# A hybrid decoder block on Trainium2: the way from output projection to gate/up rebuilt, with the memory of gate/up laid out anew

## The chip, the cores and the metric

One core of a Trainium2 chip runs the whole block in one launch. The metric is device time in microseconds (us). Lower is better.

## The reference

Input x is 1024 tokens by 1024 features in float32; there is one layer, with D_FF = 2816.

```
n = _rmsnorm(h, pre_mix_gain[l])
proj = jnp.einsum('bsd,dc->bsc', n, w_in[l])
...
merged = jnp.concatenate([_rmsnorm(a_out, out_norm_a_gain[l]),
                          _rmsnorm(b_out, out_norm_b_gain[l])], axis=-1)
mix = jnp.einsum('bsc,cd->bsd', merged, w_out[l])
h = h + _rmsnorm(mix, post_mix_gain[l])
n2 = _rmsnorm(h, pre_ffn_gain[l])
gu = jnp.einsum('bsd,df->bsf', n2, w_ffn_in[l])
ff = jax.nn.silu(gu[..., :D_FF]) * gu[..., D_FF:]
ff = jnp.einsum('bsf,fd->bsd', ff, w_ffn_out[l])
h = h + _rmsnorm(ff, post_ffn_gain[l])
```

a_out is a gated MLP with position mixing in chunks of 128 tokens, b_out a causal attention with forget gates. The change touches neither.

## The kernel before

**Arithmetic.** Every large product is made in three matmuls on numbers split into a high and a low part: `split` (L112) lets ACT write the rounded high part and DVE the rest, and `mm3` (L117) issues high x high, high x low (the moving operand's low part) and low x high. Names that end in h and l are these parts.

**Stages.** Input projections and attention come first. The output projection follows, token tile by token tile of 128, in the order 0, 1, 6, 7, 2, 4, 3, 5 (L901 to L931). For each tile `merge_start` loads its a and b halves (tile ab), `merge_norm`, `merge_a` and `merge_b` norm, transpose and split them into mh and ml, `mix_chain` makes the two output halves in PSUM (mx), and `mix_tail` (L640) norms them, adds them to x (tile xt), norms the sum again (tile tmp) and stores h. These tiles live in eight slots vs0 to vs7 that the attention's values leave free.

**Gate/up as seven products.** The norm's result and the weights of gate/up are each taken as 2 x 2 blocks, and the 2 x 2 block product is made with seven products of sums in place of eight products. The sums on the side of the activations are the forms n11, n12, n22 (blocks) and s1 to s4 (sums), each 4 x 128 rows by 512 tokens. Token tiles are paired as (0, 6), (1, 7), (2, 4), (3, 5): `norm2_first` (L828) transposes the first tile of a pair and splits n11 and n12, `norm2_second` (L834) transposes the second and makes s1 to s4 and n22. s1 and n22 are split into their forms at once. s2, s3 and s4 go to DRAM (sd) for the first three token pairs, since their place is still taken, and are reloaded before gate/up through three stage buffers (L1003); the fourth token pair is split directly.

**Pairs.** D_FF is covered by 22 steps f, called pairs here, of 128 gate and 128 up columns. `pair_raw` loads a pair's weight blocks (graw), `pair_first` splits two of them (fa), `pair_sums` makes sums (ts), `pair_split` splits these (fbc_0 and fbc_1), `pair_last` splits the fourth block (fd). PE then makes the products in the order 1, 2, 6, 5, 7, 3, 4, each with 4 x 3 = 12 matmuls of 128 x 512. Product 1 opens PSUM bank guA, 2 is guE, 6 adds to guA, 5 opens guC, 7 adds to guA, 3 to guC, 4 to guA. `snapshot` (ACT) copies guA after product 6 (u0), guC after product 5 (u1) and guA after product 7. This order is written out by hand in `pair_start`, `pair_mid` and `pair_end` (L957 on), and the loop at L1083 puts the next pair's loads, sums and splits between them.

```
wform[f, 2], wform[f, 1] = [(hi[:, j], lo[:, j]) for j in range(2)]    # fa
for i, p in enumerate(((6, 5), (7, 4))[j]): wform[f, p] = (hi[:, i], lo[:, i])    # fbc_j
wform[f, 3] = (hi[:, 0], lo[:, 0])    # fd
USES = {1: "n11", 2: "n12", 3: "s4", 4: "n22", 5: "s1", 6: "s2", 7: "s3"}
```

**Memory.** Tiles are allocated from two stacks: the left one grows from the low addresses of each partition, the right one from the high end. Before, the left stack holds s1, n22, n11, n12 and the raw weights and fa of even pairs; the right one holds s2, s3, s4, fbc_0, fbc_1 (three buffers together), fd, ts and the raw weights and fa of odd pairs. So products 5 (s1 with fbc_0) and 4 (n22 with fbc_1) have operands in both stacks in all pairs, and 1 and 2 (n11 and n12 with fa) in odd pairs.

After gate/up the down projection (L1118 on) is made with the same seven products.

## Time and profile before

| what | value |
|---|---|
| runs | 1154.29, 1154.11, 1152.98 us; median 1154.11 |
| profiled execution | 1152.77 us, of which the span is 1151.0 us |
| mean granted clock | 0.99 |
| PE, DVE, ACT, POOL busy | 96%, 63%, 45%, 15% of the span |

The span is what the profile covers, from the first to the last recorded work; the profiled execution's own time is 1.8 us longer. A busy share is an average over the whole span. "Granted clock" is the share of full speed that TensorE was given. A row of the timeline names the engine, the source line, the operation, output<-inputs, and in brackets how long the engine idled before it and what ended that.

### The profile page before, as it was taken

The numbers are of one execution on the slowest core, as the hardware profiler recorded it, in microseconds if no ns is written. First come the engines' busy times: TensorE is split into PE (matmuls) and PEld (weight loads), VectorE is DVE, ScalarE is ACT, GpSimd is POOL, SyncE is SP. The second block draws the span as 40 slices with busy tenths as digits, with TensorE's granted clock in tenths as the row PEclk, the third lists the DMA queues.
The fourth block names the chain that finished last, engine by engine and source line by source line (L and its number), as shares of the span: only waits on it lengthen the run. The fifth ranks groups of instructions, "written<-read, shape, count | busy, mean of one in ns | idle before, by whom it ended". The sixth has DMA issues, their size and how long they took to land.

```text
span 1151.0 us, 15645 instructions
## 1 busy us (share of the span) xinstructions
PE 1110.7 (96%) x5421; PEld 917.1 (80%) x5421; DVE 723.1 (63%) x1288; ACT 512.3 (45%) x989; POOL 176.8 (15%) x247
## 2 busy tenths in 40 slices
...
GB/s 262 60 92 2 83 64 120 83 93 119 75 120 174 115 232 148 110 183 237 204 253 148 181 185 240 161 183 183 230 169 141 198 302 224 196 191 196 197 199 172
DMA packets 85953, 187.76 MB, mean 163 GB/s; under 512 B 9905, under 2 KB 28401, under 8 KB 83058
## 3 DMA queue, kind: packets, MB, share of 16 engines
...
q8 instruction: 43, 0.70, 0.2%
...
## 4 chain that ended last, share of the span: by engine, by line
PE 58%; DVE 2%; issue 1%; POOL 1%; DMA 1%; ACT 1%; DVEq 0%; POOLq 0%; SPq 0%; ACTq 0%
PE guA L118 7%; PE guA L119 7%; PE guA L120 7%; PE guC L120 4%; PE guC L119 4%; PE guC L118 4%; PE dA L118 3%; PE dA L120 3%; PE dA L119 3%; PE dC L118 3%; PE dC L119 3%; PE dC L120 3%; PE guE L118 2%; PE guE L119 2%; PE guE L120 2%; PE mx L120 2%
## 5 line engine op out<-in xcount | busy, mean ns | idle before, releaser
L1141 POOL TENSOR_TENSOR y<-c,gpo 128x512 f32<-128x512 f32 x12 | 20.5, 1734 | 610.2 <-DMA dwr<-ws_d 490.5
L115 DVE TENSOR_TENSOR dal<-dar,dah 128x512 fp32r<-128x512 f32 x77 | 56.4, 733 | 88.2 <-ACT dah L114 88.2
L114 ACT CAST dah<-dar 128x512 fp32r<-128x512 f32 x77 | 48.0, 623 | 104.3 <-PE dC L119 45.8
L119 PE MATMUL dA<-dwl,dah 128*128 128x512 f32 x176 | 70.1, 398 | 2.9 <-DVE dwl L115 2.9
L118 PE MATMUL dA<-dwh,dah 128*128 128x512 f32 x176 | 69.9, 397 | 2.3 <-ACT dah L114 2.3
L120 PE MATMUL dA<-dwh,dal 128*128 128x512 f32 x176 | 69.7, 396 | 0.0
L473 POOL TENSOR_SCALAR sm<-cb,csq 128x128 f32<-128x128 f32 (+3 forms) x64 | 50.3, 787 | 90.2 <-PE pt L508 77.5
L497 ACT ACTIVATE sm<-sm,st 128x128 f32<-128x128 f32 (+3 forms) x64 | 50.0, 781 | 27.7 <-DVE st L493 27.4
L115 DVE TENSOR_TENSOR ptl<-pt,pth 128x512 fp32r<-128x512 f32 (+2 forms) x96 | 51.7, 553 | 10.4 <-ACT pth L114 9.8
L115 DVE TENSOR_TENSOR dwl<-dwr,dwh 128x512 fp32r<-128x512 f32 x77 | 55.4, 720 | 3.2 <-ACT dwh L114 3.2
L114 ACT CAST pth<-pt 128x512 fp32r<-128x512 f32 (+2 forms) x96 | 43.7, 477 | 27.6 <-PE pt L508 27.3
L115 DVE TENSOR_TENSOR fbc_1l<-ts,fbc_1h 128x1024 fp32r<-128x1024 f32 x22 | 26.9, 1225 | 45.9 <-ACT fbc_1h L114 45.9
L118 PE MATMUL qk<-nth,qkw 128*128 128x512 f32 x128 | 53.5, 419 | 0.5 <-DVE k L115 0.4
L118 PE MATMUL mx<-woh,mh 128*128 128x512 f32 x128 | 51.3, 401 | 2.5 <-ACT mh L114 2.5
L491 PE MATMUL s<-k,qu 128*128 128x384 f32 (+4 forms) x192 | 51.1, 365 | 1.5 <-DVE st L493 1.3
L120 PE MATMUL mx<-woh,ml 128*128 128x512 f32 x128 | 50.5, 397 | 1.2 <-DVE ml L115 1.2
L118 PE MATMUL dC<-dwh,dah 128*128 128x512 f32 x132 | 51.3, 389 | 0.0
L119 PE MATMUL dC<-dwl,dah 128*128 128x512 f32 x132 | 51.3, 389 | 0.0
L120 PE MATMUL dC<-dwh,dal 128*128 128x512 f32 x132 | 51.3, 389 | 0.0
L947 ACT COPY u<-guA 128x512 f32<-128x512 f32 x44 | 25.8, 585 | 56.7 <-PE guA L120 56.7
L120 PE MATMUL qk<-nth,qkw 128*128 128x512 f32 x128 | 50.5, 395 | 0.1
L119 PE MATMUL qk<-ntl,qkw 128*128 128x512 f32 x128 | 50.4, 394 | 0.0
...
## 6 DMA issues: line engine op xcount, KB each, us to landing
...
```

The source lines that it names most:

```text
L114: nc.scalar.copy(out=hi, in_=src)
L115: (lo_eng or nc.vector).tensor_tensor(out=lo, in0=src, in1=hi.bitcast(F32), op=ALU.subtract)
L118: nc.tensor.matmul(o, ah, bh, start=first, stop=False, **kw)
L119: nc.tensor.matmul(o, ah, bl, start=False, stop=False, **kw)
L120: nc.tensor.matmul(o, al, bh, start=False, stop=last, **kw)
L473: nc.gpsimd.tensor_scalar(out=sm[:, :n], in0=cbs[hh][:, :n], scalar1=csq[:, hh * NT + i:hh * NT + i + 1], scalar2=1.0, op0=ALU.add, op1=AL ...
L491: nc.tensor.matmul(o[:, :w], qu[:, hl, ts], ks_[hh][:, ks], start=hl == 0, stop=hl == 1)
L497: nc.scalar.activation(sm[:, :n], sm[:, :n], AF.Exp, bias=m, scale=-1.0, accum_out=ssum)
L947: nc.scalar.copy(out=s, in_=o)
L1141: eng.tensor_tensor(out=y[:, cs], in0=src, in1=gpo[:, cs], op=ALU.mult)
```

## The change

**Memory of gate/up.** The left stack now holds s1, s2, n11, n12, fbc_0 (pool wr, one buffer, in the place of the two gains of the norms) and fa of even and odd pairs (pool wq). The right one holds n22, s4, s3, fbc_1 (two buffers), fd, ts and the raw weights (two buffers). Products 1, 2, 6 and 5 then have both operands in the left stack, 7, 3 and 4 both in the right one.

**Output projection to gate/up.** The vs slots are given by a tile's place in the order: xt in 6 and 7, ab in 0 and 1, mh and ml in 2 to 5. The raw weights of pairs 0 and 1 are loaded in halves into slots that come free (`raw_early`), and `pair_first` for both runs before the end of the output projection. The first norm2 step of the last token pair is put inside the last tile's `mix_chain`, and the last `mix_tail` works in halves (`fine`). In `norm2_second` s1 and s2 are split at once, and n22, s4 and s3 go to DRAM; they are reloaded in the order s3, s4, n22. Between product 1 and product 2 of pair 1 the last `norm2_second` is made.

The diff, with unchanged lines left out:

```diff
--- before.py
+++ after.py
+ORDER = [0, 1, 6, 7, 2, 4, 3, 5]
 ...
     def x_load(t):
-        xts[t] = flat(vs_tile(t % 2, f"xt_{t}"))
+        xts[t] = flat(vs_tile(6 + ORDER.index(t) % 2, f"xt_{t}"))
         nc.sync.dma_start(out=xts[t], in_=x[t * P:(t + 1) * P, :])
 ...
-    def mix_tail(t, gains):
+    def mix_tail(t, gains, fine=False):
         oo, xt = [mixo[t, dh] for dh in range(2)], xts[t]
 ...
                                            op0=ALU.mult, op1=ALU.mult)
+        if fine:
+            ss = small(2, "sq")
+            cc = [slice(dh * 512, dh * 512 + 512) for dh in range(2)]
+            for dh, cs in enumerate(cc):
+                nc.vector.tensor_tensor(out=xt[:, cs], in0=xt[:, cs], in1=tmp[:, cs], op=ALU.add)
+                nc.scalar.activation(tmp[:, cs], xt[:, cs], AF.Square, scale=D ** -0.5, accum_out=ss[:, dh:dh + 1])
+            nc.sync.dma_start(out=h_d[t * P:(t + 1) * P, :], in_=xt)
+            r = rstd2(ss)
+            for cs in cc:
+                nc.vector.scalar_tensor_tensor(out=tmp[:, cs], in0=xt[:, cs], scalar=r, in1=gains[1][:, cs],
+                                               op0=ALU.mult, op1=ALU.mult)
+            normed[t] = tmp
+            return
         nc.vector.tensor_tensor(out=xt, in0=xt, in1=tmp, op=ALU.add)
 ...
-    FORMS1, FORMS2 = (("s1", "n22"), ("n11", "n12")), ("s2", "s3", "s4")
+    FORMS1, FORMS2 = (("s1", "s2"), ("n11", "n12")), ("n22", "s4", "s3")
 ...
+    forms = form_tiles(f1_cms[0].__enter__(), FORMS1[0])
+    wr_cm = pool("wr")
+    wr = wr_cm.__enter__()
+    forms.update(form_tiles(f1_cms[1].__enter__(), FORMS1[1]))
+    wq_cm = pool("wq")
+    wq = wq_cm.__enter__()
     sr_cm = pool("sr")
     sr_pools = [(sr_cm.__enter__(), 3)]
 ...
-    forms = {}
-    for cm, names in zip(f1_cms, FORMS1):
-        forms.update(form_tiles(cm.__enter__(), names))
-    wq_cm = pool("wq")
-    wq = wq_cm.__enter__()
-    mx_cm = pool("mix")
-    mx = mx_cm.__enter__()
-    gains = [mx.tile([P, D], F32, tag=nm, name=nm) for nm in ("gpm", "gpf")]
+    gains = [wr.tile([P, D], F32, tag=f"fb0{hl}", name=nm) for hl, nm in (("h", "gpm"), ("l", "gpf"))]
     load_gains(gains)
 ...
     def merge_start(t):
-        a = ab[t] = flat(vs_tile(2 + t % 2, f"ab_{t}"))
+        a = ab[t] = flat(vs_tile(ORDER.index(t) % 2, f"ab_{t}"))
         rows = slice(t * P, (t + 1) * P)
 ...
         b21, b22 = n2_transposed(t, 0, "X"), n2_transposed(t, 1, "O")
-        s1, s2, s3, s4 = [kview(s_tile(f"s{j}_{i}")) for j in range(1, 5)]
-        nc.scalar.copy(out=s1, in_=b21)
-        nc.vector.tensor_tensor(out=s3, in0=b11, in1=s1, op=ALU.subtract)
-        nc.vector.tensor_tensor(out=s1, in0=s1, in1=b22, op=ALU.add)
+        s3, s1, s2, s4 = [kview(s_tile(f"s{j}_{i}")) for j in (3, 1, 2, 4)]
+        nc.scalar.copy(out=s3, in_=b21)
+        nc.vector.tensor_tensor(out=s1, in0=s3, in1=b22, op=ALU.add)
         nc.vector.tensor_tensor(out=s2, in0=s1, in1=b11, op=ALU.subtract)
+        n2_split("s2", s2, cs)
+        n2_split("s1", s1, cs)
+        nc.vector.tensor_tensor(out=s3, in0=b11, in1=s3, op=ALU.subtract)
         nc.vector.tensor_tensor(out=s4, in0=b12, in1=s2, op=ALU.subtract)
         if last:
-            for nm, src in (("s1", s1), ("s2", s2), ("s3", s3), ("s4", s4), ("n22", b22)):
+            for nm, src in (("s3", s3), ("s4", s4), ("n22", b22)):
                 n2_split(nm, src, cs)
             return
-        n2_split("s1", s1, cs)
-        n2_split("n22", b22, cs)
-        for d, src in zip(sd, (s2, s3, s4)):
+        n22 = kview(s_tile(f"n22_{i}"))
+        nc.scalar.copy(out=n22, in_=b22)
+        for d, src in zip(sd, (n22, s4, s3)):
             nc.sync.dma_start(out=d[:, :, cs], in_=src)
 ...
     raws, wform = {}, {}
-    p1_pools = [wq]
+
+    def raw_early(f, half, slot):
+        r = raws[f, half] = flat(vs_tile(slot, f"graw_early_{f}_{half}")).rearrange("p (a w) -> p a w", a=2)
+        nc.sync.dma_start(out=r, in_=io["w_gu"][f, :, 2 * half:2 * half + 2, :])
 ...
     def pair_raw(f):
-        raws[f] = p1_pools[f % 2].tile([P, 4, 512], F32, tag="raw", name=f"graw_{f}", bufs=1)
+        raws[f] = p1.tile([P, 4, 512], F32, tag="raw", name=f"graw_{f}", bufs=2)
         nc.sync.dma_start(out=raws[f], in_=io["w_gu"][f])
+
+    def block(f, i, n=1):
+        if f in raws:
+            return raws[f][:, i:i + n, :]
+        return raws[f, i // 2][:, i % 2:i % 2 + n, :]
 ...
     def pair_first(f):
-        hi, lo = two(p1_pools[f % 2], "fa", f"fa_{f}")
-        split(as_forms(raws[f][:, 0:2, :]), hi, lo)
+        hi, lo = two(wq, f"fa{f % 2}", f"fa_{f}")
+        split(as_forms(block(f, 0, 2)), hi, lo)
         wform[f, 2], wform[f, 1] = [(hi[:, j], lo[:, j]) for j in range(2)]
 ...
     def pair_sums(f):
-        r = raws[f]
-        ts = p1_pools[1].tile([P, 4, 512], F32, tag="ts", name=f"ts_{f}", bufs=1)
-        nc.vector.tensor_tensor(out=ts[:, 1:3, :], in0=r[:, 2:4, :], in1=r[:, 1:3, :], op=ALU.subtract)
-        nc.vector.tensor_tensor(out=ts[:, 0, :], in0=r[:, 3, :], in1=ts[:, 1, :], op=ALU.subtract)
-        nc.vector.tensor_tensor(out=ts[:, 3, :], in0=r[:, 0, :], in1=ts[:, 0, :], op=ALU.subtract)
+        ts = p1.tile([P, 4, 512], F32, tag="ts", name=f"ts_{f}", bufs=1)
+        sub = lambda i, n, a, b: nc.vector.tensor_tensor(out=ts[:, i:i + n, :], in0=a, in1=b, op=ALU.subtract)
+        if f in raws:
+            sub(1, 2, block(f, 2, 2), block(f, 1, 2))
+        else:
+            sub(1, 1, block(f, 2), block(f, 1))
+            sub(2, 1, block(f, 3), block(f, 2))
+        sub(0, 1, block(f, 3), ts[:, 1:2, :])
+        sub(3, 1, block(f, 0), ts[:, 0:1, :])
         raws[f, "t"] = ts
 ...
     def pair_split(f, j):
-        hi, lo = two(p1_pools[1], "fbc", f"fbc_{f}_{j}", bufs=3)
+        hi, lo = two(*((p1, "fb1") if j else (wr, "fb0")), f"fbc_{f}_{j}", bufs=1 + j)
         split(as_forms(raws[f, "t"][:, 2 * j:2 * j + 2, :]), hi, lo)
 ...
     def pair_last(f):
-        hi, lo = two(p1_pools[1], "fd", f"fd_{f}", 1)
-        split(as_forms(raws[f][:, 3:4, :]), hi, lo)
+        hi, lo = two(p1, "fd", f"fd_{f}", 1)
+        split(as_forms(block(f, 3)), hi, lo)
         wform[f, 3] = (hi[:, 0], lo[:, 0])
 ...
     merge_start(order[2])
 ...
     for i, t in enumerate(order):
+        if i == 7:
+            raw_early(0, 1, 2)
         if i >= 2:
-            for _ in mix_chain([(t, 0, KALL, "mm"), (t, 1, KALL, "S")]):
-                pass
+            for step, _ in enumerate(mix_chain([(t, 0, KALL, "mm"), (t, 1, KALL, "S")])):
+                if i == 7 and step == 4:
+                    pair_first(1)
+                if i == 7 and step == 11:
+                    norm2_first(3)
         if i in (3, 4, 6):
 ...
             merge_norm(t2, ab[t2][:, AW:], gb, junk)
-        if i == 7:
-            norm2_first(3)
         if i >= 2:
-            mix_tail(t, gains)
+            mix_tail(t, gains, i == 7)
         if i + 2 < NT:
             x_load(t2)
-            k = 4 + 2 * (i % 2)
+            k = 2 + 2 * (i % 2)
             merged[t2] = (vs_tile(k, f"mh_{t2}"), vs_tile(k + 1, f"ml_{t2}"))
 ...
             merge_start(order[i + 4])
-        if i == 4:
-            pair_raw(0)
+        if i in (4, 5):
+            raw_early(i - 4, 0, i - 4)
+        if i == 5:
             pair_first(0)
-    mx_cm.__exit__(None, None, None)
+    sr_cm.__exit__(None, None, None)
     gb_cm.__exit__(None, None, None)
 ...
-    p1_cm = pool("p1", side="right")
-    p1_pools.append(p1_cm.__enter__())
     f2_cm = pool("f2p", side="right")
     f2p = f2_cm.__enter__()
-    sr_pools.append((p1_pools[1], 3))
+    forms.update(form_tiles(f2p, FORMS2))
+    p1_cm = pool("p1", side="right")
+    p1 = p1_cm.__enter__()
+    sr_pools[0] = (p1, 6)
 ...
     def open_bank(f, which):
-        state[f, which] = bank(BANKS[which], f"gu{which}_{f}")
+        state[f, which] = bank("S" if (f, which) == (0, "C") else BANKS[which], f"gu{which}_{f}")
         return state[f, which]
 ...
-    def pair_start(f):
+    def pair_start(f, between=None):
         a = open_bank(f, "A")
 ...
         g0 = state[f, "g0"] = snapshot(a, f"g0_{f}")
+        if between:
+            between()
         e = open_bank(f, "E")
 ...
-    pair_raw(1)
-    pair_first(1)
-    pair_sums(0)
-    pair_split(0, 0)
-    forms.update(form_tiles(f2p, FORMS2))
-    pair_start(0)
-    pair_start(1)
-    for nm, d in zip(FORMS2, sd):
+    def reload(nm, d):
         for j in range(2):
 ...
             split(w, forms[nm][0][:, ks, :384], forms[nm][1][:, ks, :384])
-    norm2_second(3, True)
+
+    pair_sums(0)
+    pair_last(0)
+    pair_raw(1)
+    pair_start(0)
+    pair_split(0, 0)
+    pair_start(1, lambda: norm2_second(3, True))
     pair_split(0, 1)
-    pair_last(0)
+    for nm, d in reversed([*zip(FORMS2, sd)]):
+        reload(nm, d)
 ...
```

In steady pairs PE's order is the same as before. Three places where it, or DVE's, is another:

PE at the end of the output projection, before (mx are the output banks, tp_n_3 the transposes of tile 3's norm, guA and guE the first banks of pair 0):

```order
L119 MATMUL mx_1_5571<-wol_4411,mh_5421 128x512
L120 MATMUL mx_1_5571<-woh_4410,ml_5422 128x512
L818 MATMUL tp_n_3_0_5596<-ident,tmp_5527 128x128 x4
L818 MATMUL tp_n_3_1_5601<-ident,tmp_5527 128x128 x4
L118 MATMUL guA_5659<-n11h,fa_0h 128x512
L118 MATMUL guE_5674<-n12h,fa_0h 128x512
L119 MATMUL guA_5659<-n11l,fa_0h 128x512
```

and with the change:

```order
L119 MATMUL mx_1_5585<-woh_4361,mh_5421 128x512
L120 MATMUL mx_1_5585<-wol_4362,mh_5421 128x512
L831 MATMUL tp_n_3_0_5598<-ident,tmp_5535 128x128 x4
L831 MATMUL tp_n_3_1_5603<-ident,tmp_5535 128x128 x4
L121 MATMUL mx_1_5585<-woh_4361,ml_5422 128x512
L119 MATMUL mx_1_5585<-woh_4410,mh_5421 128x512
L120 MATMUL mx_1_5585<-wol_4411,mh_5421 128x512
L121 MATMUL mx_1_5585<-woh_4410,ml_5422 128x512
L119 MATMUL guA_5673<-n11h,fa_0h 128x512
L120 MATMUL guA_5673<-n11l,fa_0h 128x512
```

The transposes of tile 3 now stand ahead of the last four matmuls of the output projection, and the first product of pair 0 follows these without a transpose between; its matmuls are no longer mixed with those of guE.

DVE at the end of tile 3's output projection, before (xt is x plus the mix, tmp the norms' result, n11l to n22l forms, s_2 the sums of the third token pair):

```order
L649 SCALAR_TENSOR_TENSOR tmp_5527<-mx_0_5437,st_303_5533,gpm 128x512
L115 TENSOR_TENSOR n11l<-tp_n_2_0_5487,n11h 128x4x128
L115 TENSOR_TENSOR n12l<-tp_n_2_1_5492,n12h 128x4x128
L841 TENSOR_TENSOR s_2_5513<-tp_n_2_0_5487,s_2_5511 128x512
L649 SCALAR_TENSOR_TENSOR tmp_5527<-mx_1_5462,st_303_5533,gpm 128x512
L842 TENSOR_TENSOR s_2_5511<-s_2_5511,tp_n_4_1_5506 128x512
L651 TENSOR_TENSOR xt_5318<-xt_5318,tmp_5527 128x1024
L843 TENSOR_TENSOR s_2_5512<-s_2_5511,tp_n_2_0_5487 128x512
L115 TENSOR_TENSOR s1l<-s_2_5511,s1h 128x4x128
L844 TENSOR_TENSOR s_2_5514<-tp_n_2_1_5492,s_2_5512 128x512
L115 TENSOR_TENSOR n22l<-tp_n_4_1_5506,n22h 128x4x128
L107 TENSOR_SCALAR st_305_5541<-st_304_5539 128x1
```

and with the change:

```order
L650 SCALAR_TENSOR_TENSOR tmp_5535<-mx_0_5443,st_303_5541,gpm 128x512
L116 TENSOR_TENSOR n11l<-tp_n_2_0_5493,n11h 128x4x128
L116 TENSOR_TENSOR n12l<-tp_n_2_1_5498,n12h 128x4x128
L854 TENSOR_TENSOR s_2_5518<-s_2_5517,tp_n_4_1_5512 128x512
L650 SCALAR_TENSOR_TENSOR tmp_5535<-mx_1_5468,st_303_5541,gpm 128x512
L855 TENSOR_TENSOR s_2_5519<-s_2_5518,tp_n_2_0_5493 128x512
L116 TENSOR_TENSOR s1l<-s_2_5518,s1h 128x4x128
L858 TENSOR_TENSOR s_2_5517<-tp_n_2_0_5493,s_2_5517 128x512
L116 TENSOR_TENSOR s2l<-s_2_5519,s2h 128x4x128
L859 TENSOR_TENSOR s_2_5520<-tp_n_2_1_5498,s_2_5519 128x512
L665 TENSOR_TENSOR xt_5322<-xt_5322,tmp_5535 128x1024
L108 TENSOR_SCALAR st_305_5549<-st_304_5547 128x1
```

The residual add into xt and the scaling into tmp (L665 and L670, before L651 and L656) now come after the sums and splits of s1 and s2. Before, the add stood ahead of four of them.

PE in the second half of pair 0, before (guC takes product 3, guA products 7 and 4):

```order
L119 MATMUL guA_5659<-s3l,fbc_1h 128x512
L120 MATMUL guA_5659<-s3h,fbc_1l 128x512
L118 MATMUL guC_5809<-s4h,fd_0h 128x512
L119 MATMUL guC_5809<-s4l,fd_0h 128x512
L120 MATMUL guC_5809<-s4h,fd_0l 128x512
```

and with the change:

```order
L121 MATMUL guC_5823<-s4h,fd_0l 128x512
L119 MATMUL guC_5823<-s4h,fd_0h 128x512
L121 MATMUL guE_6016<-n12h,fa_2l 128x512
L120 MATMUL guC_5823<-s4l,fd_0h 128x512
L121 MATMUL guC_5823<-s4h,fd_0l 128x512
L119 MATMUL guC_5823<-s4h,fd_0h 128x512
L120 MATMUL guC_5823<-s4l,fd_0h 128x512
L121 MATMUL guC_5823<-s4h,fd_0l 128x512
L119 MATMUL guA_5673<-n22h,fbc_1h 128x512
L119 MATMUL guE_6016<-n12h,fa_2h 128x512
L120 MATMUL guA_5673<-n22l,fbc_1h 128x512
L121 MATMUL guA_5673<-n22h,fbc_1l 128x512
```

Single matmuls of pair 2's second product (guE with fa_2) now stand between those of pair 0's products 3 and 4.

## Rows read from the trace of the kernel before

**Rows 1.** The page, busy us (share of the span) x instructions of PE.
```profile
PE 1110.7 (96%) x5421; PEld 917.1 (80%) x5421; DVE 723.1 (63%) x1288; ACT 512.3 (45%) x989; POOL 176.8 (15%) x247
```

**Rows 2.** Busy time by stretch: us, PE, PEld, DVE, ACT, POOL, PEclk, DMA share, GB/s.
```profile
485.20:536.70 51.50, 43.67 (x185) 33.88 (x184) 45.84 (x60) 28.76 (x42) 1.09 (x2) 0.93 0.59 198
536.70:923.70 387.00, 387.00 (x1682) 314.88 (x1682) 245.88 (x318) 141.57 (x203) 0.00 (x0) 1.00 0.56 195
```

**Rows 3.** Timeline of PE at product starts: start us, us, engine line op, [idle before <-releaser].
```profile
536.75 0.40 PE L118 MATMUL guA<-n11h,fa_2h 128*128 128x512 f32 x1
...
691.52 0.40 PE L118 MATMUL guA<-n11h,fa_10h 128*128 128x512 f32 x1
...
694.27 0.39 PE L118 MATMUL guE<-n12h,fa_10h 128*128 128x512 f32 x1
...
696.99 0.39 PE L118 MATMUL guA<-s2h,fbc_0h 128*128 128x512 f32 x1
...
710.81 0.39 PE L118 MATMUL guA<-n11h,fa_11h 128*128 128x512 f32 x1
...
713.61 0.39 PE L118 MATMUL guE<-n12h,fa_11h 128*128 128x512 f32 x1
...
716.41 0.39 PE L118 MATMUL guA<-s2h,fbc_0h 128*128 128x512 f32 x1
...
923.68 0.40 PE L118 MATMUL dA<-dwh,dah 128*128 128x512 f32 x1
```

**Rows 4.** Timeline of PE, 485 to 505 us.
```profile
485.18 1.03 PE L818 MATMUL tp_n<-ident,tmp 128*128 128x128 f32 x8
...
486.59 0.49 PE L118 MATMUL guA<-n11h,fa_0h 128*128 128x512 f32 x1 [0.38 <-ACT n11h L114]
...
488.44 0.50 PE L119 MATMUL guA<-n11l,fa_0h 128*128 128x512 f32 x1 [0.87 <-DVE n11l L115]
...
494.43 0.41 PE L818 MATMUL tp_n<-ident,tmp 128*128 128x128 f32 x2 [0.71 <-DVE tmp L656]
...
501.25 0.80 PE L118 MATMUL guA<-n11h,fa_1h 128*128 128x512 f32 x1 [5.75 <-ACT fa_1h L114]
...
504.52 0.39 PE L118 MATMUL guA<-n11h,fa_1h 128*128 128x512 f32 x1
```

**Rows 5.** Timeline of ACT in pair 10.
```profile
702.52 1.05 ACT L114 CAST fbc_1h<-ts 128x1024 fp32r<-128x1024 f32 x1 [1.98 <-PE guC L119]
703.47 0.58 ACT L947 COPY u<-guC 128x512 f32<-128x512 f32 x1
```

**Rows 6.** Timeline of DVE: tails of tile 3 (478 to 483) and tile 5 (489 on).
```profile
478.07 1.22 DVE L651 TENSOR_TENSOR xt<-xt,tmp 128x1024 f32<-128x1024 f32 x1
...
479.20 0.68 DVE L843 TENSOR_TENSOR s<-s,tp_n 128x512 f32<-128x512 f32 x1
...
481.01 0.68 DVE L115 TENSOR_TENSOR n22l<-tp_n,n22h 128x512 fp32r<-128x512 f32 x1
...
482.48 1.28 DVE L656 SCALAR_TENSOR_TENSOR tmp<-xt,st,gpf 128x1024 f32<-128x1024 f32 x1 [0.73 <-POOL st L109]
...
489.68 1.22 DVE L651 TENSOR_TENSOR xt<-xt,tmp 128x1024 f32<-128x1024 f32 x1
...
493.00 1.28 DVE L656 SCALAR_TENSOR_TENSOR tmp<-xt,st,gpf 128x1024 f32<-128x1024 f32 x1 [0.73 <-POOL st L109]
```

**Rows 7.** Groups of the page and timeline of ACT: a DVE split, an ACT copy.
```profile
L115 DVE TENSOR_TENSOR fbc_1l<-ts,fbc_1h 128x1024 fp32r<-128x1024 f32 x22 | 26.9, 1225 | 45.9 <-ACT fbc_1h L114 45.9
...
496.26 0.59 ACT L840 COPY s<-tp_n 128x512 f32<-128x512 f32 x1
```

**Rows 8.** DMA issues: out<-in, queue, count, KB each, median us to landing.
```profile
re_s<-sd_s SPq DMA_DIRECT2D x6, 384.0 KB, 3.7
```

**Rows 9.** Timeline of PE in the output projection.
```profile
453.03 0.52 PE L127 MATMUL tp_ma<-ident,ab 128*128 128x128 f32 x3 [0.36 <-issue]
...
462.20 0.55 PE L127 MATMUL tp_mb<-ident,ab 128*128 128x128 f32 x3 [0.75 <-DVE ab L601]
```

More of the change, by code (lines that the diff above doesn't have):

```diff
@@ L771, in hybrid_block @@
     at_cm.__exit__(None, None, None)
-    FORMS1, FORMS2 = (("s1", "n22"), ("n11", "n12")), ("s2", "s3", "s4")
-    sr_cm = pool("sr")
-    sr_pools = [(sr_cm.__enter__(), 3)]
+    FORMS1, FORMS2 = (("s1", "s2"), ("n11", "n12")), ("n22", "s4", "s3")
     f1_cms = [pool("f1a"), pool("f1b")]
@@ L782, in form_tiles @@
         return {nm: [pl.tile([P, HALF, 512], F32R, tag=f"{nm}{hl}", name=f"{nm}{hl}") for hl in "hl"] for nm in names}
-    forms = {}
-    for cm, names in zip(f1_cms, FORMS1):
-        forms.update(form_tiles(cm.__enter__(), names))
+    forms = form_tiles(f1_cms[0].__enter__(), FORMS1[0])
+    wr_cm = pool("wr")
+    wr = wr_cm.__enter__()
+    forms.update(form_tiles(f1_cms[1].__enter__(), FORMS1[1]))
     wq_cm = pool("wq")
     wq = wq_cm.__enter__()
-    mx_cm = pool("mix")
-    mx = mx_cm.__enter__()
-    gains = [mx.tile([P, D], F32, tag=nm, name=nm) for nm in ("gpm", "gpf")]
+    sr_cm = pool("sr")
+    sr_pools = [(sr_cm.__enter__(), 3)]
+    gains = [wr.tile([P, D], F32, tag=f"fb0{hl}", name=nm) for hl, nm in (("h", "gpm"), ("l", "gpf"))]
     load_gains(gains)
```

6 lines of the change are left out of this document (3 added, 3 removed).

## The prediction

> **What bounds the kernel now.** I began with the page's first part: TensorE (PE) is busy for 96% of the span [rows 1]. The kernel ends when PE ends, so a change is worth what it does to PE's idle time or to the pace of its matmuls. The table by stretches says which of the two is to be had where [rows 2]: in the 387.0 us of gate/up pairs 2 to 21 PE is busy for 387.0, so only the pace can change; in the 51.5 us before them, which hold the last norm and pairs 0 and 1, it is busy for 43.7 at a granted clock of 0.93, so there idle time is to be had.
>
> Next PE's own timeline, at pair starts [rows 3]. Twenty pairs take 923.68 - 536.75 = 386.93 us, 19.35 each. Pair 10 takes 710.81 - 691.52 = 19.29, so an odd pair takes 19.40. The reader should compare one product in both: gate/up's second product (guE, 12 matmuls) takes 696.99 - 694.27 = 2.72 us in pair 10 and 716.41 - 713.61 = 2.80 in pair 11. What differs is where its weights lie: fa_10 in the left stack beside n12, fa_11 in the right one. I read this as a price for operands that meet across the halves: 226.7 ns a matmul on one side, 233.3 across, 0.08 us a product. Two or four crossed products in a pair should then add 0.16 or 0.32 to 84 x 0.2267 = 19.04; the rows say 0.25 and 0.36. Roughly 0.03 to 0.04 seems to go when PE passes from a product on one side to one on the other (pair 10's first product takes 694.27 - 691.52 = 2.75 after one on the right, the second 2.72).
>
> Last, PE's waits between the last output-projection matmul and pair 2 [rows 4]. From 485.18 to 536.75 are 51.57 us. The work in it is two groups of 8 transposes at 1.03 and 168 matmuls at 0.2267, 2.1 + 38.1 = 40.2; so 11.4 us are lost. The rows place 10.4 of them: 0.38 and 0.87 for n11 with two matmuls 0.49 long between them (0.5 lost), 0.71 for tmp, 5.75 for fa_1, then seven matmuls from 501.25 to 504.52 in 3.27 us for 1.59 (1.7, after the idle time the pace is that of the lower clock level), and 72 crossed matmuls (0.5). The remaining 1.0 is in waits under 0.3.
>
> **The change, part by part.**
>
> *Memory.* In pairs 2 to 21 no instruction moves on PE. Products 1, 2, 6, 5 come to lie wholly left and 7, 3, 4 wholly right, in this order, so that PE changes sides twice a pair. I take 19.04 + 2 x 0.04 = 19.12 a pair: 19.35 - 19.12 = 0.227, times 20 is **4.5 us**. Bounds: 1.1 if odd pairs only fall to what even ones take now (10 x 0.11), 6.1 if every pair falls to 19.04 (20 x 0.307). I take the middle value since guE of pair 10 shows the floor itself.
>
> The Trainium skill ("SBUF — State Buffer", section "Who interferes with whom") says "PE and ACT never wait on anyone": by it an operand's place would be worth nothing, and this term would be 0 instead of 4.5. The trace disagrees, 2.72 against 2.80 us for the same product, unless something else goes with odd pairs; that is the first rival below.
>
> fbc_0 now has one buffer where three served fbc_0 and fbc_1. ACT's cast of the next fbc_0h must wait for product 5, which reads the old one last. It costs nothing, because the cast in this place already waits for product 5 today [rows 5]: at 702.52 the cast of fbc_1h starts after 1.98 us of idling for guC, and the u1 copy behind it runs 703.47 to 704.05. Product 3, which writes the bank that the copy reads, comes only after product 7, at about 702.5 + 2.72 = 705.2. Cover: 1.1 us a pair.
>
> *The order from output projection to pair 2.* Weights of pairs 0 and 1 are loaded in halves into freed vs slots, and both fa tiles are split before the last tile's output projection ends. That removes the 5.75 wait and its 1.7 of slow matmuls. The gains' reload and the s copies stay off PE's path. What the new order waits for instead, walked by hand:
> - The transposes of tile 3 stand before the last four mx matmuls, so PE wants them 4 x 0.227 before 485.18, at 484.27. DVE, however, now makes four more 0.60 us steps before tile 3's residual add (rows 479.20 to 481.01 of [rows 6] are three such steps in 1.81): the add starts at 478.07 + 2.4 = 480.5; from add to scale the last tile takes 493.00 - 489.68 = 3.3, so the scale runs 483.8 to 485.1 instead of 482.48 to 483.76. PE waits **0.85**.
> - Then 1.03 of transposes and four mx matmuls to 487.0, with the n11 and n12 splits running beside the latter: the 0.38 and 0.87 go. First products of pair 0, second of pair 0 and first of pair 1 are 36 x 0.227 = 8.2, to 495.2. tmp of the last tile is ready by about 495 (494.28 now, and the halves add two short steps): the 0.71 goes.
> - Transposes to 496.2, pair 1's second product to 498.9. Product 5 of pair 0 wants s1: ACT's copy 0.59, DVE's add 0.6, then the 1.23 of fbc_1l that stands between, s2 0.6 and s1l 0.7 [rows 6, 7] give about 500.1. PE waits **1.2**.
> - s3, s4 and n22 come back from DRAM through three stage buffers. The first s4 load can be issued only when a buffer is free, after s3's split at about 505.3; with 3.7 to land [rows 8] and a split of 768 elements (three quarters of the 1.05 and 1.23 of 1024 elements [rows 5, 7], 1.7, and 0.3 between the engines) it is there at 511.0, and PE wants it at 510.2: **0.8**. n22, behind it on the same queue, 0 to 1.0; I take **0.3**.
> - In these waits PE does four matmuls of pair 2 (0.9), which it needs not do later.
>
> New waits 0.85 + 1.2 + 0.8 + 0.3 = 3.15, less 0.9; the changes of side 0.2; of the small waits I let 0.5 stand. So the gain is 11.4 - 3.15 + 0.9 - 0.2 - 0.5 = **8.5 us**. Bounds: all 11.4, and 4.8 if one reload of the chain lands a whole 3.7 us later than walked.
>
> *Output projection.* ab and xt change slots with the tile's place in the order rather than its number, which lets loads go out earlier. PE waits there now 0.36 and 0.75 [rows 9] on ab: at most 1.1, at least 0; I take **0.7**, the larger one.
>
> The sum is 4.5 + 8.5 + 0.7 = 13.7 us. It is made from an execution of 1152.77 us (span 1151.0 and 1.8 around it), 0.12% under the median of the runs, 1154.11; taken from the median it gives **1140.4**.
>
> **The rivals.**
> - *The side of an operand is worth nothing*, and odd pairs are slow by something else that stays. Without the 4.5 and the 0.5 in pairs 0 and 1 the time is 1154.1 - 8.7 = 1145.4. For: even pairs cross too and the rows show only 0.11 between the two. Against: the one product that changes sides between pairs is the one that changes its time. This rival is what the Trainium skill's page "SBUF — State Buffer" would have here.
> - *The reload chain takes the place of fa_1.* Three stage buffers carry six loads of 3.7 us that a split must free in turn. One missed turn brings an idle stretch like that at 501.25 with its slow matmuls, 3.7 + 1.7 = 5.4: 1145.8; if nothing of the 8.5 is left, 1148.9. For: slack at s4 is already negative in my walk. Against: the same six loads are covered now with as many buffers.
> - *Not all operands are moved*: if two products of every odd pair still meet across, 10 x 2 x 0.08 = 1.6 are missing: 1142.0. The stacks meet near the middle, so a tile could lie astride; nothing in the profile tells.
> - *Slower: fbc_0's only buffer.* The place is ACT between products 5 and 3. If cast and u1 copy come later than their 1.1 cover, product 3 waits in every pair, on the otherwise gapless 387 us. To eat the 13.7 the delay must be 1.1 + 13.7/20 = 1.8 us in each pair; with 2.0 it would be 1154.1 - 13.7 + 20 x 0.9 = 1158.4. For: three buffers become one. Against: ACT idles for 1.98 us just there.
>
> **How the numbers follow.** My forecast has 0.70, the worthless side 0.09, the reload chain 0.14, unmoved operands 0.03, the slower one 0.04. The likeliest case's own range is 1137 to 1145. The whole range begins at 1135.5, all three upper bounds (6.1 + 11.4 + 1.1), and reaches up over the worthless side and the reload chain to 1148.5, leaving out part of the latter and the slower case. What a measurement can tell from no change is about 0.2%, 2.3 us: all cases but the last lie further below 1154.1. I give faster 0.93, same 0.03 (a reload chain worse than its bound, with a cover of fbc_0 just gone), slower 0.04.
>
> **What the changed profile would show.** Right: pairs 2 to 21 in 382 to 383 us, odd and even alike, guE of an odd pair in 2.72; no idle time of 5 us before guA<-n11h,fa_1h; waits of about 1 us before s1 and s4; pair 2 starting near 528 to 529 on the old clock. Wrong on the sides: 386 to 387 us for twenty pairs. Wrong on the reload: idle time over 3 us released by re_s splits, and a clock under 1.00 behind it. Wrong altogether: PE idle in every pair before guC<-s4h.

## The result, and the profile after

The changed kernel takes 1140.16 us (median of 4 runs, 1139.41 to 1142.65), the kernel before 1153.55 (4 runs); the ratio is 0.9884 with a 95% interval of 0.9869 to 0.9899. Forecast were 1140.4 us. (Below, two numbers behind a ratio are such an interval; the ratio is to the kernel before.) The profiled execution took 1140.83 us, its span is 1138.8 (1152.77 and 1151.0 before).

From the page after, the line that answers to [rows 1], and from the table by stretches the two lines that answer to [rows 2]; the stretches begin at the first transposes of tile 3 and at pair 2:

```profile
PE 1102.8 (97%) x5421; PEld 915.8 (80%) x5421; DVE 722.2 (63%) x1291; ACT 515.2 (45%) x994; POOL 177.7 (16%) x247
...
487.00:531.70 44.70, 42.91 (x189) 33.76 (x188) 40.80 (x57) 28.03 (x43) 1.79 (x2) 1.00 0.62 210
531.70:912.70 381.00, 381.00 (x1678) 314.62 (x1677) 249.32 (x323) 142.00 (x203) 0.00 (x0) 1.00 0.58 198
```

In the way to pair 2 PE is now busy for 42.9 of 44.7 us at full clock, where it was 43.7 of 51.5 at 0.93. In pairs 2 to 21 it is busy throughout, as before, and 6 us shorter. (0.9 of these 6 are matmuls of pair 2 that now stand among pair 0's.)

PE's timeline at product starts of pairs 10 and 11, the counterpart of [rows 3]:

```profile
683.56 0.39 PE L119 MATMUL guA<-n11h,fa_10h 128*128 128x512 f32 x1
...
686.29 0.39 PE L119 MATMUL guE<-n12h,fa_10h 128*128 128x512 f32 x1
...
689.01 0.39 PE L119 MATMUL guA<-s2h,fbc_0h 128*128 128x512 f32 x1
...
702.65 0.39 PE L119 MATMUL guA<-n11h,fa_11h 128*128 128x512 f32 x1
...
705.38 0.39 PE L119 MATMUL guE<-n12h,fa_11h 128*128 128x512 f32 x1
...
708.10 0.39 PE L119 MATMUL guA<-s2h,fbc_0h 128*128 128x512 f32 x1
```

Even and odd pairs are alike: 702.65 - 683.56 = 19.09 us, and product 2 takes 2.72 in both (689.01 - 686.29 and 708.10 - 705.38), where the odd pair took 2.80. Product 1 takes 2.73.

What PE waited for from 440 to 535 us (engine, line, releaser: total, times, longest):

```profile
PE tp_ma L128 <- issue: 1.4, 1, 1.4
PE guC L120 <- DVE s1l L116: 1.0, 1, 1.0
PE tp_n L831 <- DVE tmp L670: 0.9, 1, 0.9
PE guA L119 <- ACT u L979: 0.7, 1, 0.7
PE tp_n L831 <- DVE st L108: 0.2, 1, 0.2
```

The 5.75 for fa_1 [rows 4] is gone, and so are the slow matmuls behind it. The waits for tile 3's tmp (0.9) and for s1l (1.0) are where the forecast put them. tp_ma waits longer than before (1.4 against 0.36 [rows 9]), and a wait before product 4 of pair 1 (0.7) is new.

Stage by stage, from PE's timeline of both profiled executions:

| stage | forecast | measured |
|---|---|---|
| output projection, to the last tile's first matmul | -0.7 | +0.8 |
| from there to pair 2 | -8.5 | -7.1 |
| pairs 2 to 21 | -4.5 | -5.1 (19.35 to 19.09 a pair) |
| outside of the changed stages | 0 | -0.8 |
| sum | -13.7 | -12.2 |

The output projection is counted from tile 6's first matmul (404.13 before, 404.57 after) to the last tile's (474.16, 475.35). The four matmuls of pair 2 that stand among pair 0's, 0.9 us, are counted with pairs 2 to 21. Outside, the stages ahead are 0.4 longer and what follows gate/up is 1.2 shorter; this was not followed.

The slowest and the fastest run of one kernel lie 1.5 to 5.4 us apart here, in one case 7.6 (best7), so the runs below that change a wait of 1 us are read in their traces, not by their medians.

### The profile page after: what moved, and what is told of

Same layout as the page of the kernel before. It is cut to its first block, busy times and chain, and to the rows that moved or that the text cites. A ratio compares the mean times of both kernels' runs of the same rounds, so it can differ in the third digit from the quotient of the medians.

```text
span 1138.8 us, 15652 instructions
## 1 busy us (share of the span) xinstructions
PE 1102.8 (97%) x5421; PEld 915.8 (80%) x5421; DVE 722.2 (63%) x1291; ACT 515.2 (45%) x994; POOL 177.7 (16%) x247
## 4 chain that ended last, share of the span: by engine, by line
PE 54%; DVE 4%; issue 2%; DMA 2%; POOL 1%; ACT 1%; SPq 0%; DVEq 0%; POOLq 0%; ACTq 0%
PE guA L119 7%; PE guA L121 6%; PE guA L120 6%; PE guC L119 3%; PE guC L120 3%; PE guC L121 3%; PE dA L119 3%; PE dA L120 3%; PE dA L121 3%; PE dC L120 3%; PE dC L119 3%; PE dC L121 3%; PE guE L120 2%; PE guE L121 2%; PE guE L119 2%
## 5 line engine op out<-in xcount | busy, mean ns | idle before, releaser
L115 ACT CAST pth<-pt 128x512 fp32r<-128x512 f32 (+2 forms) x96 | 43.7, 477 | 27.4 <-PE pt L509 27.1
L116 DVE TENSOR_TENSOR fbc_0l<-ts,fbc_0h 128x1024 fp32r<-128x1024 f32 x22 | 26.9, 1223 | 38.8 <-ACT fbc_0h L115 38.8
L120 PE MATMUL mx<-wol,mh 128*128 128x512 f32 x128 | 50.2, 392 | 0.0
```

What stands on the lines that cost most here:

```text
L115: nc.scalar.copy(out=hi, in_=src)
L116: (lo_eng or nc.vector).tensor_tensor(out=lo, in0=src, in1=hi.bitcast(F32), op=ALU.subtract)
L120: nc.tensor.matmul(o, ah, bl, start=False, stop=False, **kw)
```

## The experiments

### Where an operand lies

**fa_right** keeps the new order and lays fa back across the stacks.

```diff
 def pair_raw(f):
-    raws[f] = p1.tile([P, 4, 512], ...)
+    pl, tag = (p1, "fr1") if f == 1 else (wq, f"fa{f % 2}")    # two halves
 def pair_first(f):
-    hi, lo = two(wq, f"fa{f % 2}", f"fa_{f}")
+    hi, lo = two(*((p1, f"fr{f % 2}") if f > 1 else (wq, f"fa{f % 2}")), f"fa_{f}")
...
+    pair_raw(1)    # moved ahead of pair_sums(0)
```

> From pair 2 on the weights fa of products 1 and 2 lie in the right stack (odd pairs at 122.8 to 131.0 thousand bytes, even pairs at 172 to 180), and the raw weights in their place in the left one; n11 and n12 stay left at 72 to 105 thousand. Theory (operands that meet across the two halves cost 6.7 ns a matmul, wherever in the half they lie): product 2 takes 2.80 us in place of 2.72 in every pair from 2 on, a pair about 19.25 in place of 19.10, together +3 us. Rival 1 (it is the distance between the two operands, not a border): 2.80 in even pairs only, 2.72 in odd ones, together +1.5 us. Rival 2 (an operand's place is worth nothing): 2.72 and 19.10 in all pairs, +0.

Measured: 1144.21 us (ratio to before 0.9909, 0.9888 to 0.9931), 4 us over the changed kernel. PE's timeline, product 2 of pairs 10 and 11 and the product behind it:

```profile
690.68 0.39 PE L119 MATMUL guE<-n12h,fa_10h 128*128 128x512 f32 x1
...
693.48 0.40 PE L119 MATMUL guA<-s2h,fbc_0h 128*128 128x512 f32 x1
...
709.95 0.39 PE L119 MATMUL guE<-n12h,fa_11h 128*128 128x512 f32 x1
...
712.75 0.40 PE L119 MATMUL guA<-s2h,fbc_0h 128*128 128x512 f32 x1
```

2.80 us in both, and 709.95 - 690.68 = 19.27 a pair. fa_11 lies at 122.8 thousand bytes, next to the left stack's end, and costs what fa_10 costs at 172. So it is a border and not the distance, and both rivals fall. The raw weights went left in exchange; products 3, 4 and 5, whose operands stayed, still take 2.72 (product 3 of pair 10 starts at 701.71, product 4 at 704.43), so the price goes with the operands of products 1 and 2 and not with the raw weights.

**fd_left** asks where the border is.

```diff
-    hi, lo = two(p1, "fd", f"fd_{f}", 1)
+    hi, lo = two(wd, "fd", f"fd_{f}", 1)    # wd: a left pool above wq; the last pair's in p1
```

> The weights fd of product 3 lie in the left stack's upper end, at 121.2 to 125.3 thousand bytes, and s4 stays right at 196 to 213 thousand. Theory (a price across a border that lies above the left stack's end): product 3 takes 2.80 us in place of 2.72, and a pair 0.08 to 0.16 more, together +1.6 to +3 us. Rival (distance): 2.72, +0; then the same place is near enough to both stacks.

One run: 1140.92 us. PE's timeline, product 3 of pair 10 and the product behind it:

```profile
696.68 0.39 PE L119 MATMUL guC<-s4h,fd_10h 128*128 128x512 f32 x1
...
699.43 0.39 PE L119 MATMUL guA<-n22h,fbc_1h 128*128 128x512 f32 x1
```

2.75 us, a third of the price of 0.08, between the theory's 2.80 and the rival's 2.72. By start times the eight matmuls with fd_10h (121.2 to 123.3 thousand) take 229 to 232 ns, about half of the 6.7 ns more that a crossed matmul took above, and the four with fd_10l (from 123.3 thousand) 226. The reading that fd_10h lies left of the border and fd_10l right of it fits, but it is argued: why the price is only half is open. The border itself follows better from fa_11, which pays in full where it begins at 122.8 thousand (fa_right) and nothing where it ends at 121.2 (the changed kernel): for weights it lies near 122 thousand bytes. The byte is not settled.

### The 5.75 us for fa_1

**fa1_late** takes the early load of pair 1 away.

```diff
-                if i == 7 and step == 4:
-                    pair_first(1)
...
-        if i in (4, 5):
-            raw_early(i - 4, 0, i - 4)
+        if i == 4:
+            raw_early(0, 0, 0)
...
+    pair_raw(1)
+    pair_first(1)
     pair_sums(0)
     pair_last(0)
-    pair_raw(1)
     pair_start(0)
```

> Pair 1's raw weights are loaded and split where the kernel before did it, after the output projection; the rest is the changed kernel. Theory (early weights are what shortened the way to pair 2): before the first matmul of pair 1 PE idles 4 to 6 us for fa_1 again, with matmuls at the lower clock behind it, and the kernel is 5 to 7.5 us slower. Rival (the other waits of the new order, 0.9 and 1.0 and 0.7, run under it, and the reordering was the gain): under 4 us slower.

Measured: 1142.26 us (0.9895, 0.9872 to 0.9917); in the trace pair 2's products come 2.0 us later than in the changed kernel, counted from the last tile's first matmul. The theory falls, the rival's bound holds. ACT's timeline shows why:

```profile
493.41 1.03 ACT L115 CAST fa_1h<-graw 128x1024 fp32r<-128x1024 f32 x1
494.35 1.04 ACT L115 CAST fbc_0h<-ts 128x1024 fp32r<-128x1024 f32 x1
...
497.30 1.28 ACT L999 ACT_TABLE_LOAD   x1
```

The late load goes out at 487.4, has landed 5.5 us later and is there for a cast at 493.4. In the kernel before, SP's and ACT's timelines were:

```profile
491.31 0.43 SPq L860 DMA_DIRECT2D graw<-in_w_gu  x1
```

```profile
497.39 1.28 ACT L967 ACT_TABLE_LOAD   x1
...
499.22 1.03 ACT L114 CAST fbc_0h<-ts 128x1024 fp32r<-128x1024 f32 x1
500.15 1.04 ACT L114 CAST fa_1h<-graw 128x1024 fp32r<-128x1024 f32 x1
```

There the load landed 5.7 us after its issue, at 497.0, and the cast stood behind those of fd_0 and fbc_0, the table load and the silu, at 500.15. So two bounds stood one behind the other: the load held the cast until 497.0, ACT's order for 3.1 us more. By these rows, as an estimate, the load alone would still have left about 2.6 of the 5.75 us (497.0 and 1.1 from cast to matmul, less 495.5, where PE began to idle). fa1_late takes both away, since its load goes out ahead of the store of h and its cast stands first on ACT. (In the changed kernel only the first half of pair 1's raw weights is loaded early; the whole block is loaded again at 488.0.)

**before_hd** asks from the other side whether the load was late, in the kernel before.

```diff
-            mix_tail(t, gains)
+            mix_tail(t, gains, nc.scalar if i == 7 else nc.sync)    # the queue of h's store
```

> The kernel before, with one edit: the store of the last tile's h is issued from ACT's queue in place of SP's, so that the load of pair 1's raw weights no longer stands behind it. Theory (what made pair 1 wait 5.75 us was a load behind a store on SP's queue, not the place in memory and not the order of the splits): the load goes out 4 to 6 us earlier, PE's idle time before the first matmul of pair 1 falls under 2 us, the slow matmuls behind it go, and the kernel is 4 to 7 us faster than before. Rival (ACT's own order, where the cast of fa_1 stands behind the casts of fbc_0 and the silu, holds it): the load goes out earlier, but the idle time stays above 4 us, and under 2 us are gained.

Measured: 1155.15 us (1.0003, 0.9991 to 1.0015). From SP's and ACT's timelines:

```profile
488.65 0.46 SPq L860 DMA_DIRECT2D graw<-in_w_gu  x1
```

```profile
501.53 0.63 ACT L967 ACTIVATE g<-g 128x512 f32<-128x512 f32 x1
502.06 1.03 ACT L114 CAST fa_1h<-graw 128x1024 fp32r<-128x1024 f32 x1
```

The load goes out at 488.65 and has landed 5.8 us later, at 494.4, and its cast waits for ACT's order until 502.06. PE idles 5.3 us, little less than the 5.75. The rival holds: with the load in time, ACT's order alone keeps the wait.

**fa1_behind** is fa1_late with the cast forced behind the silu.

```diff
+    pair_silu(0)
+    pair_first(1, state[0, "g0"])
...
+        if after is not None:
+            nc.scalar.copy(out=hi[:, 0].rearrange("p k c -> p (k c)"), in_=after)
```

> As fa1_late, but ACT copies pair 0's silu result into fa_1h just ahead of its cast, so that this cast must stand behind the silu and its table load on ACT, as it does in the kernel before. The load of pair 1's raw weights goes out as early as in fa1_late. Theory (the 5.75 us came from the place of fa_1's cast in ACT's order): PE idles 4 to 8 us for fa_1h before pair 1's first product, with slow matmuls behind it, and the kernel is 6 to 10 us slower than fa1_late. Rival (the load decides, and it is there in time): under 2 us slower.

Measured: 1151.88 us (0.9981, 0.9971 to 0.9991), 9.6 over fa1_late. ACT's and PE's timelines:

```profile
498.49 0.63 ACT L1001 ACTIVATE g<-g 128x512 f32<-128x512 f32 x1
...
501.00 1.04 ACT L115 CAST fa_1h<-graw 128x1024 fp32r<-128x1024 f32 x1
```

```profile
502.09 0.79 PE L119 MATMUL guA<-n11h,fa_1h 128*128 128x512 f32 x1 [4.45 <-ACT fa_1h L115]
502.68 0.63 PE L120 MATMUL guA<-n11l,fa_1h 128*128 128x512 f32 x1
```

The load is as early as in fa1_late (487.7); the idle time and the 0.63 us matmuls are back, with a granted clock of 0.60 from 502 to 510 us. The theory holds. Not all of the 9.6 is the cast: tmp of the last tile is late too (2.7), since engine orders were made anew. What the change gained here is a place in ACT's order together with a load that is issued in time; splitting the weights before the last norm adds the 2.0 us of fa1_late. No run has the load at its old time with the cast ahead on ACT.

### The output projection

**s3_first** and **tail_s3** move DVE's steps.

```diff
 s3_first
         nc.vector.tensor_tensor(out=s2, in0=s1, in1=b11, op=ALU.subtract)
+        if not last:
+            (s3 and s4 here, in place of behind the two n2_split)
 tail_s3: also
+        if i == 6:
+            norm2_second(2)    # behind mix_tail, in place of ahead
```

> The changed kernel, with s3 and s4 made before s1 and s2 are split in the first three norm2_second. Theory (tp_ma of tile 3 waits 1.36 us for a PSUM bank, whose last reader the change has moved behind the splits): the wait falls under 0.4 us, and the stretch up to the last tile is 1.0 us shorter. Rival (it waits for its load): 1.36 us stay.

Measured: 1140.89 us (0.9881, 0.9863 to 0.9898). tp_ma still waits 1.4, and the stretch up to the last tile is 0.2 us shorter, not 1.0. It starts 0.1 us after the last reader of the transposed block b11 ends, in the kernel before (452.93, 453.03), in the changed one (454.41, 454.51) and here (454.68, 454.77): the bank is what it waits for, and not its load, which in the changed kernel had landed at 424.9. But the edit brought that reader only one step forward, and DVE began the group late.

> As s3_first, and tile 3's mix_tail stands ahead of the last early norm2_second. Theory (tp_n_3 waits 0.86 us since six steps on DVE stand ahead of tile 3's residual add): that wait goes too, 1.9 us less than the changed kernel up to pair 0. Rival (then tp_n_3 waits for the banks that the second norm now holds longer): the wait stays near 0.9 us or grows, and nothing is gained over s3_first.

Measured: 1141.63 us (0.9897, 0.9874 to 0.992). The 0.86 before tp_n_3 is gone, and PE's timeline has in its place:

```profile
498.73 1.53 PE L831 MATMUL tp_n<-ident,tmp 128*128 128x128 f32 x7 [1.93 <-DVE tmp L661]
```

The steps moved behind tile 3's tail now delay the last tile's. Up to pair 0 0.9 us are gained, not 1.9, and this wait takes more than that back. Neither theory nor rival named it.

**ab_parity** asks why DVE was late.

```diff
-        a = ab[t] = flat(vs_tile(ORDER.index(t) % 2, f"ab_{t}"))
+        a = ab[t] = flat(vs_tile(t % 2, f"ab_{t}"))
```

> The changed kernel with ab's two slots given by the tile's parity, as before. Theory (the earlier load of the last tile's ab put its multiply on GpSimd ahead of tile 7's rstd, which waited 1.85 us, and the delay ran on to tile 3's transposes): the 1.85 us on DVE before tile 7's scaling fall to about 0.7, tp_ma's 1.36 falls by 0.5 to 1.2, while the wait of 0.75 before tp_mb of the last tile comes back; from the first matmul of tile 6 to the last tile's first it is 0 to 0.7 us shorter. Rival (the new order of the second norm alone delays DVE): 1.36 stays.

Measured: 1141.09 us (0.9892, 0.9873 to 0.991). First GpSimd's and DVE's timelines of the changed kernel, then DVE's and PE's waits of ab_parity:

```profile
444.27 1.05 POOL L598 TENSOR_TENSOR ab<-ab,rsum 128x512 f32<-128x512 f32 x1 [4.81 <-DMA ab<-bo_d]
445.27 0.55 POOL L110 TENSOR_TENSOR st<-st,mhalf 128x1 f32<-128x1 f32 x1
```

```profile
445.86 1.28 DVE L670 SCALAR_TENSOR_TENSOR tmp<-xt,st,gpf 128x1024 f32<-128x1024 f32 x1 [1.85 <-POOL st L110]
```

```profile
443.56 1.28 DVE L670 SCALAR_TENSOR_TENSOR tmp<-xt,st,gpf 128x1024 f32<-128x1024 f32 x1 [0.66 <-POOL st L110]
```

```profile
PE tp_mb L128 <- DVE ab L602: 2.2, 1, 2.2
...
PE tp_ma L128 <- issue: 0.4, 1, 0.4
```

In the changed kernel the last tile's ab is loaded earlier, its multiply stands ahead of tile 7's rstd on GpSimd, and waits 4.8 us for the load. The rstd behind it is 1.2 late, and so is all of DVE's chain up to b11's last reader. With the old slots this goes and tp_ma waits 0.4; but the last tile's ab then comes 2.2 late, not 0.75. The stretch is 1.1 us longer than in the changed kernel. The mechanism holds, the price of its cure was wrong. The timelines of GpSimd and DVE in ab_parity show 1.0 us of the difference:

```profile
457.63 2.02 POOL L598 TENSOR_TENSOR ab<-ab,rsum 128x512 f32<-128x512 f32 x1 [0.20 <-issue]
```

```profile
457.46 1.28 DVE L670 SCALAR_TENSOR_TENSOR tmp<-xt,st,gpf 128x1024 f32<-128x1024 f32 x1 [0.73 <-POOL st L110]
```

The multiply of the last tile's ab takes 2.02 us, where it took 1.05 in the changed kernel (above) and 1.04 in the kernel before, and ends 0.9 after DVE's scaling beside it. In the kernel before that scaling had ended 1.9 us before the multiply began; by the new order of the second norm the residual add and this scaling stand behind the sums.

**best5** and **best7** put cures together.

```diff
 best5: tail_s3, and
+        nc.vector.tensor_tensor(out=s2, in0=b22, in1=s3, op=ALU.subtract)    # s3 ahead of s2
-    pair_split(0, 1)
+    pair_split(0, 1, nc.gpsimd)
     (pair_last(1) ahead of pair_split(1, 1); pair 1's sums block by block)
 best7: ab_parity, s3_first, and pair_last(1) ahead of pair_split(1, 1)
```

> As tail_s3, and: s2 is made from s3 so that it does not wait for s1, the low part of pair 0's fbc_1 is made on GpSimd, and pair 1's fd is split before its fbc_1, so that the buffer of pair 3's raw weights comes free earlier. Theory (the 0.74 us before product 4 of pair 1 is ACT's u copy behind a cast that waits for that load): this wait goes, s1's wait of 0.97 shrinks by 0.3 to 0.7, and 3 us are gained on the changed kernel, about 1137 us. Rival (GpSimd's subtraction of 128x1024 is late for product 7 of pair 0): a new wait of over 1 us stands there.

Measured: 1140.77 us (0.9882, 0.9865 to 0.99), not 1137. The wait before product 4 falls to 0.3 and product 7 does not wait, but s1h and s1l wait 1.1 and 1.3 us. The timelines of GpSimd and DVE, and DVE's same step in the changed kernel:

```profile
495.44 2.95 POOL L116 TENSOR_TENSOR fbc_1l<-ts,fbc_1h 128x1024 fp32r<-128x1024 f32 x1 [0.75 <-ACT fbc_1h L115]
```

```profile
496.66 2.82 DVE L116 TENSOR_TENSOR fbc_0l<-ts,fbc_0h 128x1024 fp32r<-128x1024 f32 x1
```

```profile
497.73 1.21 DVE L116 TENSOR_TENSOR fbc_0l<-ts,fbc_0h 128x1024 fp32r<-128x1024 f32 x1
```

DVE's subtraction takes 2.82 us in place of 1.21: it ends 1.1 after GpSimd's, as if it began only then. What was taken off DVE stopped DVE. The Trainium skill ("SBUF — State Buffer", section "Who interferes with whom") says that a VectorE instruction with two inputs in SBUF contends with a GpSimd instruction that reads SBUF; the trace agrees, 1.6 us. In ab_parity DVE's scaling was first, and GpSimd's multiply was the one that took longer.

> As ab_parity, with s3 and s4 made ahead of the splits in the first three norm2_second, and pair 1's fd split ahead of its fbc_1. Theory: both of tile 3's waits shrink, and the 0.74 us before product 4 of pair 1 goes: 1 to 2 us off the changed kernel in the stretch from tile 6 to pair 3. Rival (DVE, busy for over nine tenths of that stretch, sets its length): under 0.5 us.

Measured: 1140.03 us (0.9891, 0.9862 to 0.9919). The wait before product 4 of pair 1 is gone, and from the last tile's first matmul to pair 3 it is 1.3 us shorter than the changed kernel. But the output projection before that is 2.4 longer: tp_mb's wait of 2.2 is there as in ab_parity, with a multiply of 2.09 us, and behind it the granted clock is 0.76 from 463 to 470 us, with matmuls 0.43 us apart for 0.227, the pace of the lower clock level. In ab_parity the clock did not fall behind the same wait; why is open. So pair 3 starts 1.1 us later, counted from tile 6's first matmul. No version tried beats the changed kernel beyond what runs differ by.

### The slower rival

**act_more** and **u1_more** load ACT between products 5 and 3.

```diff
 act_more, in pair_split
+        for _ in range(2 * (j == 0 and f > 2)):
+            nc.scalar.copy(out=hi, in_=as_forms(raws[f, "t"][:, 0:2, :]))
 u1_more, in pair_mid
+        for _ in range(4 if f > 2 else 0):
+            nc.scalar.copy(out=u1, in_=c)
```

> From pair 3 on ACT makes the cast into fbc_0h three times in place of once, 1.9 us more between product 5 and the copy of its bank. Theory (the one buffer of fbc_0 leaves 1.2 us of cover before product 3): product 3 waits 0.65 to 0.75 us in each of 19 pairs, +12 to +14 us. Rival 1 (no cover, the cast is already on the path): +36 us. Rival 2 (all hidden): +0.

Measured: 1140.71 us (0.9879, 0.9857 to 0.99), no cost. ACT's timeline of pair 10:

```profile
695.35 1.05 ACT L911 CAST fbc_0h<-ts 128x1024 fp32r<-128x1024 f32 x1 [1.91 <-PE guC L120]
696.31 0.58 ACT L981 COPY u<-guC 128x512 f32<-128x512 f32 x1
696.78 1.05 ACT L911 CAST fbc_0h<-ts 128x1024 fp32r<-128x1024 f32 x1
```

The build put the u1 copy behind the first cast and the others behind the copy, so the run did not delay what it was to delay. u1_more ties the load to the copy itself.

> From pair 3 on ACT copies product 5's bank five times in place of once; fbc_0h's cast stands ahead of these copies. Theory (about 1.2 us of cover between the u1 copy and product 3): cast 1.0, four copies 1.95, u3's copy and the last one 1.0 make 3.95 us after product 5's end, product 7 ends after 2.76, so product 3 starts 1.1 to 1.3 us late in each of 19 pairs, +21 to +25 us. Rival 1 (no cover): four copies of 0.49 on the path, +37 us. Rival 2 (ACT is nowhere near the path): +0.

One run: 1144.0 us. PE's timeline of pair 10:

```profile
698.60 0.39 PE L120 MATMUL guA<-n11l,fa_11h 128*128 128x512 f32 x1
698.82 0.49 PE L119 MATMUL guA<-n22h,fbc_1h 128*128 128x512 f32 x1
...
699.38 0.43 PE L119 MATMUL guC<-s4h,fd_10h 128*128 128x512 f32 x1
```

Product 3 does start about 1.7 us late, but the time is filled: the build's scheduler has put five matmuls of the next pair and two of product 4 ahead of it. A pair takes 19.28 in place of 19.09, 0.19 us, not 1.2. No theory had this. It seems that the build orders PE for the delay that it foresees; no run tests that.

## Why the prediction was right, and where not

**Memory of gate/up: right, a little small.** The price by side is shown by taking it away (19.09) and by putting part of it back (fa_right, 19.27). In the kernel before it stands at the products that crossed: in pair 10 products 5 and 4 take 2.80 (699.75 to 702.55, 708.01 to 710.81). The term that was mis-sized is the passage between sides, "roughly 0.03 to 0.04" each way, 19.12 a pair. It is 0.04 from left to right and 0.01 back (product 1, 2.73). Product 7 of pair 10 in the changed kernel shows the former:

```profile
694.45 0.39 PE L119 MATMUL guA<-s3h,fbc_1h 128*128 128x512 f32 x1
...
697.21 0.39 PE L119 MATMUL guC<-s4h,fd_10h 128*128 128x512 f32 x1
```

2.76 us; product 6 of pair 10 in the kernel before, which passes the same way, takes 2.76 too (696.99 to 699.75). So 5.1 us and not 4.5. What a passage is stays open: the extra time is spread over the first ten matmuls of product 7. The rival by which a side is worth nothing is excluded. The Trainium skill's sentence ("SBUF — State Buffer", section "Who interferes with whom"), as the prediction read it, would have made this term 0, and the trace disagrees with that reading; the sentence itself is about engines that wait for one another, not about a matmul's own two operands.

**The way to pair 2: right in size, half right in its reason.** The step is "Weights of pairs 0 and 1 are loaded in halves into freed vs slots, and both fa tiles are split before the last tile's output projection ends. That removes the 5.75 wait". It removes it, but most of that needs neither halves nor slots nor a split so early: fa1_late, without them for pair 1, costs 2.0 us. What held the wait last was fa_1's place in ACT's order: an earlier load alone gains nothing (before_hd), and the place alone brings 4.5 us of idle time back (fa1_behind). The walk's new waits held where they came from DVE (0.86 for 0.85, 0.97 for 1.2). The 0.8 for s4 and the 0.3 for n22 did not come: matmuls of pair 2 stand there. In their place a wait came that the walk had not followed to the end, 0.74 before product 4 of pair 1:

```profile
526.31 1.05 ACT L115 CAST fa_3h<-graw 128x1024 fp32r<-128x1024 f32 x1 [3.07 <-DMA graw<-in_w_gu]
527.27 1.04 ACT L115 CAST fbc_0h<-ts 128x1024 fp32r<-128x1024 f32 x1
528.22 0.58 ACT L979 COPY u<-guA 128x512 f32<-128x512 f32 x1
```

ACT's cast of fa_3 waits for a load whose buffer came free late, and the u copy stands behind it. best7, which frees that buffer earlier, has no such wait. These three waits make 2.6 us, where the walk had 3.15 less 0.9, 2.25. So they explain 0.3 of the missing 1.4 us. The term that was too small is "of the small waits I let 0.5 stand", with 0.2 for the changes of side: what is lost outside the three waits is 1.9 us, in pieces under 0.3, and was not followed further.

**Output projection: wrong sign.** The step that failed is "ab and xt change slots [...], which lets loads go out earlier", taken as all that happens there; the new order of DVE's steps was put at nothing. The earlier load by itself gains: with ab's old slots the stretch is 1.1 us longer than in the changed kernel (ab_parity). But with ab's old slots and the rest of the change it is 1.9 longer than in the kernel before, 1.5 of it in tp_mb's wait (2.2 for 0.75). With the new slots that wait is gone, tp_ma's grows by 1.0 (1.36 for 0.36), since the earlier load drew a multiply ahead of a rstd on GpSimd, and 0.8 is left. That b11's bank is held longer by the new order of the second norm fits three traces; no run took the order away alone, so its share is argued.

**The total** came within 0.3 us, and that is luck: +1.5 in the output projection and +1.4 on the way against -0.6 in the pairs and -0.8 outside of the changed stages leave the spans 12.2 us apart in place of 13.7, and the medians happen to lie 13.4 apart. From the profiled execution of the kernel before, the same sum gives 1139.1 for the changed one; it took 1140.83.

**The slower rival** did not come. In pair 10 of the changed kernel ACT's timeline has

```profile
694.42 1.05 ACT L115 CAST fbc_0h<-ts 128x1024 fp32r<-128x1024 f32 x1 [1.91 <-PE guC L120]
695.38 0.58 ACT L979 COPY u<-guC 128x512 f32<-128x512 f32 x1
```

so the copy ends at 695.96 and product 3 starts at 697.21 (above): a cover of 1.2 us, for 1.1 forecast. Where ACT was made late, PE's order was another (u1_more).
